# Two attention mixers of a decoder trunk: keys projected ahead of queries, odd values four heads at a time, a shorter inverse root

## The chip, the cores and the metric

One core of one Trainium2 chip runs the whole kernel in one launch. The metric is device time in microseconds (us), the median of three runs.

## The reference

A decoder of two layers on a sequence of 512 tokens of width 1024, all in float32. Each layer is half a SwiGLU feed-forward block (width 2816), a mixer, and half a feed-forward block again; each part reads a root-mean-square norm of the running sum `x` and adds to it.

```python
def rms_norm(x, g):
    y = x * rsqrt(mean(x * x, axis=-1) + 1e-6)
    return y * g

x = x + 0.5 * swiglu(rms_norm(x, ffn_pre_norm[l]), ...)
h = rms_norm(x, mix_norm[l])
x = x + even_mixer(h) if l == 0 else x + odd_mixer(h)
x = x + 0.5 * swiglu(rms_norm(x, ffn_post_norm[l]), ...)

# even: z = h @ w_in; 8 heads x 64 of causal attention (with 512 tokens and blocks of 256
#   every past block is chosen), beside a gated unit of 8 groups x 64; both -> w_out
# odd: 8 heads, each with two q/k maps of 64 and values of 128:
p = softmax(causal(q k^T / 8))          # for both maps
a = p[0] - lam * p[1]
o = rms_norm(a @ v, subln_g) * (1 - lambda_init)      # -> w_out
```

q and k of every head get a rotary embedding on their first 16 dimensions. A final norm ends it.

## The kernel before

`x` lies in SBUF as 8 tiles of 128 features x 512 tokens. Every float32 operand is split into a rounded high part and a low rest (`hi`, `lo`, the format is `fp32r`), and every product is three matmuls: high times high, high times low, low times high (`mm3`). A weight chunk of 128x1024 is loaded (`w_raw`), rounded on ACT (L128) and subtracted on DVE (L129).

All work is a list of slots. One slot is a projection or a part of one; for the mixers that is 24 matmuls of 512 columns (`project`) or, for the odd values, 48 of 256 columns. `st.later(n, fn)` hangs smaller work (a head's scores, transposes, the product with the values, a norm) n slots further on; `step()` emits what is due ahead of the slot's matmuls. This sets the order in which the code is written. The framework then schedules: it may put instructions that it reckons ready ahead of earlier ones on the same engine, and each engine runs its list in order. In the trace the matmuls of the output projection stand between a head's transposes, which the code writes in one block.

In a mixer `qk_slots` projects a pair (even: two heads; odd: the two maps of one head) in two slots, queries first, then keys. `rotated` (L839 to L842) applies the rotary embedding and hands the result to `Pair.q` or `Pair.k` one step later. `Pair.q` makes for each half of the rows a tile `qs` with the high part in the half's own 64 rows and the low part in the other 64. `Pair.k` makes for each half a tile `ks` that holds high and low of the keys in both 64-row halves: round (L862), subtract (L863), and one transfer on SP's queue from the half's own rows to the other 64 (L864). `Pair.scores` (L882, L883) then needs two matmuls per 128 queries.

Numbers of slots after the queries' and keys' pair: `EV` for the even mixer (scores, transposes, product with the values), `OD` for the odd one (scores of map 0, of map 1, transposes, product, sums of squares, row scale).

The odd values are projected for two heads at a time (`values(p)`, after heads 1, 3, 5 and 7), two slots each, into two PSUM banks. The output projection (`out_proj`) follows: three `begin` slots with the first half of the contraction, then `end_early`, which takes heads' results as they become available and emits the last heads' hung-on work between; six of the eight PSUM banks hold its sums then.

`rsqrt` (L205 to L221) is the inverse root without a table: a guess from the bits, a cubic step and a Newton step, ten DVE instructions; it runs 15 times (six norms, one layer norm, eight heads).

Of the kernel before, what the change touches and what calls it, by code (L numbers as in the profile page):

```python
# [18 lines left out]
P = 128  # L19
# [13 lines left out]
def trunk_kernel(ctx: ExitStack, tc: tile.TileContext, a, out):  # L33
# [6 lines left out]
    def bank(name):  # L40
        return ps.tile([P, 512], F32, name=name, tag="bank")
# [5 lines left out]
    def t2k(tag, name, dt=F32):  # L47
        return act.tile([P, T], dt, name=name, tag=tag, bufs=BUFS[tag])
# [7 lines left out]


    EB = 3
    EV = (3, 5, 6)
    OD = (3, 4, 6, 7, 9, 10)  # L60


    class Item:
# [141 lines left out]
    def rsqrt(dst, src, scale, n, plus=EPS):  # L205


        v, y, a, b = [sm.tile([P, n], F32, name=f"rs{i}") if n <= 32 else tmp(f"rs{i}") for i in range(4)]
        if isinstance(plus, float):
            nc.vector.tensor_scalar(v, src, scale, plus, op0=OP.mult, op1=OP.add)  # L210
        else:
            nc.vector.scalar_tensor_tensor(v, src, scale, plus, op0=OP.mult, op1=OP.add)
        nc.vector.tensor_scalar(y.bitcast(I32), v.bitcast(I32), -0.5, float(0x5F3759DF), op0=OP.mult, op1=OP.add)
        nc.vector.tensor_mul(a, y, y)
        nc.vector.tensor_mul(a, a, v)
        nc.vector.tensor_scalar(b, a, 0.375, -1.25, op0=OP.mult, op1=OP.add)
        nc.vector.tensor_mul(b, b, a)
        nc.vector.scalar_tensor_tensor(y, b, 1.875, y, op0=OP.add, op1=OP.mult)
        nc.vector.scalar_tensor_tensor(a, y, -0.5, y, op0=OP.mult, op1=OP.mult)
        nc.vector.tensor_mul(a, a, v)  # L220
        nc.vector.scalar_tensor_tensor(dst, a, 1.5, y, op0=OP.add, op1=OP.mult)  # L221


    class Norm:
# [607 lines left out]
    def two(name, dt=F32):  # L832
        return w4(name, dt)

    def rotated(pq, tables, place):

        cr, sr = tables
        sw, q = tmp("sw"), tmp("q")
        nc.vector.stream_shuffle(sw, pq, SWAP)  # L839
        nc.vector.tensor_mul(q, pq, cr)  # L840
        nc.vector.tensor_mul(sw, sw, sr)
        nc.vector.tensor_add(q, q, sw)  # L842
        st.mids.append(lambda: place(q))

    class Pair:
# [10 lines left out]
                self.QS.append(t)  # L856

        def k(self, k):
            for h in range(2):
                own, other = HALF[h], HALF[1 - h]  # L860
                t = two("ks", F32R)
                nc.scalar.activation(t[own, 0], k[own], AF.Copy)  # L862
                nc.vector.tensor_sub(t[own, 1], k[own], t[own, 0].bitcast(F32))  # L863
                nc.sync.dma_start(t[other].bitcast(F32), t[own].bitcast(F32))  # L864
                self.KH.append(t[:, 0])
                self.KL.append(t[:, 1])

        def scores(self, c, su, o, ebufs):

# [93 lines left out]
    def qk_slots(w, norm, tables, pair, hold, after):  # L963

        def fn(o):
            def go(ws):
                b = bank("pq")
                project(b, ws, norm)

                def evac():  # L970
                    rotated(b, tables(), pair.q if o == 0 else pair.k)
                    if o == 1:
                        after()
                if hold:
                    st.later(hold - o, evac)
                else:
                    evac()
            return go
        st.add([chunk(w[0])], fn(0))
        st.add([chunk(w[1])], fn(1))  # L980


    def even_mixer(norm, feed):
# [170 lines left out]
    def odd_mixer(norm, feed):  # L1154
# [22 lines left out]
        def head(h, pair):  # L1177

            keep = {}

            def s0():
                keep["su"] = sm.tile([P, 2 * TT], F32, name="su2")
                keep["e0"] = pair.scores(0, keep["su"], 0, EB)

            def s1():
                su = keep["su"]
                e0, e1 = keep["e0"], pair.scores(1, su, TT, EB)
                ratio = sm.tile([P, TT], F32, name="su")
                nc.vector.reciprocal(ratio, su[:, TT:])
                nc.vector.scalar_tensor_tensor(ratio, ratio, box["neg_lam"], su[:, :TT], op0=OP.mult, op1=OP.mult)  # L1190
                for i in range(TT):
                    nc.vector.scalar_tensor_tensor(e0[i], e1[i], ratio[:, i:i + 1], e0[i],
                                                   op0=OP.mult, op1=OP.add)
                nc.vector.scalar_tensor_tensor(box["eps"][:, :, h], su[:, :TT], EPS, su[:, :TT], op0=OP.mult, op1=OP.mult)

            def t():
                keep["pt"] = transposed(keep["e0"])

            def o():
                o_ = attend(box["v", h // 2], slice((h % 2) * P, (h % 2 + 1) * P), keep["pt"])  # L1200
                keep["o"] = t2k("r2", "o")
                nc.scalar.activation(keep["o"], o_, AF.Copy)
                sq = tmp("sq")
                nc.scalar.activation(sq, o_, AF.Square)
                keep["sq"] = sq

            def c():
                pc = bank("pc")
                for t in range(TT):
                    nc.tensor.matmul(pc[:, t:t + 1], keep["sq"][:, t * P:(t + 1) * P], ones1,  # L1210
                                     start=True, stop=True)
                keep["col"] = sm.tile([P, TT], F32, name="ocol")
                rsqrt(keep["col"], pc[:, :TT], 1.0 / P, TT, box["eps"][:, :, h])

            def r():
                row = bcast_row(keep["col"], "orow", True)
                on = keep["o"]
                nc.vector.scalar_tensor_tensor(on, on, box["sg"], row, op0=OP.mult, op1=OP.mult)
                if h < 2:
                    t = two("m", F32R)  # L1220
                    mh[h], ml[h] = split_into(t[:, 0], t[:, 1], on)
                else:
                    mh[h], ml[h] = split(on, "m", "h")

            for n, fn in zip(OD, (s0, s1, t, o, c, r)):
                st.later(n + int(fn is r and h < 7), fn)

        def values(p):
            b = []

            def half(n):
                def fn(w):
                    if n == 0:
                        b.extend(bank("pv") for _ in range(2))
                    for t in range(TT):
                        r = slice(t * P, (t + 1) * P)
                        o = b[t // 2][:, (t % 2) * 256:(t % 2 + 1) * 256]
                        for k in range(4 * n, 4 * n + 4):
                            s = slice((k % 4) * 256, (k % 4 + 1) * 256)
                            go = {"skip_group_check": True}  # L1240
                            nc.tensor.matmul(o, norm.hi[k][:, r], w[0][:, s], start=k == 0 and t % 2 == 0,
                                             stop=False, **go)
                            nc.tensor.matmul(o, norm.hi[k][:, r], w[1][:, s], start=False, stop=False, **go)
                            nc.tensor.matmul(o, norm.lo[k][:, r], w[0][:, s], start=False, stop=k == KT - 1, **go)
                    if n == 1:
                        evac()
                return fn

            def evac():
                halves = [t2k("h", "v", F32R).rearrange("p (n c) -> p n c", n=2) for _ in range(3)]  # L1250
                vh = [halves[t][:, 0] for t in range(TT - 1)]
                vl = [halves[t][:, 1] for t in range(TT - 1)]
                vw = t2k("h", "vw")[:, :256]
                for t in range(TT):
                    evac_value(t, b[t // 2][:, (t % 2) * 256:(t % 2 + 1) * 256], norm.col[:, t:t + 1], vh, vl, vw)
                box["v", p] = (vh, vl, vw)
            for n in range(2):
                st.add([chunk(a["ov"][p, n])], half(n))

        for h in range(8):  # L1260
            pair = Pair()
            if h == 0:
                n = len(st.slots)
                qk_slots(a["oqk"][h], norm, lambda: box["rope"], pair, 2,
                         lambda h=h, pair=pair: head(h, pair))
                first, end, fn, dense, raws = st.slots[n]
                st.slots[n] = (first, end, lambda ws, fn=fn: (begin(), fn(ws)), dense, raws)
            else:
                qk_slots(a["oqk"][h], norm, lambda: box["rope"], pair, 0,
                         lambda h=h, pair=pair: head(h, pair))  # L1270
            if h % 2 == 1:
                values(h // 2)
        out_proj(a["oo"], ([0, 1, 2, 3], [4, 5, 6, 7]), mh, ml, feed)

# [167 lines left out]
```

## Time and profile before

| | |
|---|---|
| median of 3 runs | 1815.01 us (1814.34 to 1815.54) |
| profiled execution | 1815.92 us |
| its span, first to last instruction | 1813.9 us |
| PE (matmul) busy | 1801.5 us, 12708 matmuls |
| DVE busy | 1553.2 us |
| ACT busy | 981.2 us |
| POOL busy | 177.2 us |
| mean granted TensorE clock | 0.998 of full |

A matmul's row gives its start and its duration with the drain of the array; successive ones overlap, so the step from start to start is what a matmul costs in a stream. The profiled execution lasted 2.0 us longer than its span, and 0.9 us longer than the median of the runs.

### The profile page before, as it was taken

Reading aid. Unit: us, or ns where it says so; the run is one execution under the profiler, and the core shown is the slowest. Engines: PE = TensorE matmul, PEld = TensorE weight load, DVE = VectorE, ACT = ScalarE, POOL = GpSimd, SP = SyncE. Lnnn points to the kernel's source line nnn. Section 1 sums busy time; section 2 is a strip of 40 time slices with the busy share of each in tenths; the row PEclk is TensorE's granted clock in tenths of the full one; section 3 lists DMA queues with packets and bytes.
Section 4 is the critical chain, followed back from the end, with each engine's and each line's share of the span. In section 5 each row is a group of like instructions: output and inputs, shape, how many; then the busy total and the mean of one; then the engine's idle time right before and its main releaser. Section 6 shows DMA issues by size and latency. Waiting matters only on the chain.

```text
span 1813.9 us, 32304 instructions
## 1 busy us (share of the span) xinstructions
PE 1801.5 (99%) x12708; PEld 1689.5 (93%) x12708; DVE 1553.2 (86%) x2554; ACT 981.2 (54%) x1577; POOL 177.2 (10%) x154
## 2 busy tenths in 40 slices
PE   9999999999999999999999999999999999999998
PEld 7999999888888999999899999998999889999997
DVE  8989898878868889898988989888999688898986
ACT  6545554544965545454654646455566455455544
POOL 0111110100000111110011111100000001111100
PEclk9999999999999999999999999999999999999999
DMA  7587876421325687875547878742333245878771
GB/s 244 128 222 168 221 167 170 142 96 59 117 82 148 153 224 163 223 160 151 170 115 187 201 188 201 187 132 90 94 94 94 93 138 130 221 169 220 169 179 62
DMA packets 150743, 279.87 MB, mean 154 GB/s; under 512 B 11840, under 2 KB 65728, under 8 KB 150592
## 3 DMA queue, kind: packets, MB, share of 16 engines
q1 hardware_dynamic: 111216, 209.62, 36.2%
q0 software_dynamic: 38080, 67.12, 22.8%
q8 instruction: 100, 1.64, 0.4%
q10 hardware_dynamic: 1296, 1.08, 0.2%
q14 instruction: 51, 0.42, 0.1%
HBM read 269.39 MB, written 2.10 MB: 150 GB/s over the span
## 4 chain that ended last, share of the span: by engine, by line
PE 96%; DVE 2%; ACT 1%; issue 0%; DMA 0%; SPq 0%; DVEq 0%
PE pA L417 11%; PE pA L416 11%; PE pA L415 11%; PE pD L415 6%; PE pD L417 6%; PE pD L416 6%; PE pB L417 3%; PE pB L416 3%; PE pB L415 3%; PE py L180 3%; PE py L182 3%; PE py L181 3%; PE pq L181 2%; PE pq L182 2%; PE pq L180 2%; PE pu L182 2%
## 5 line engine op out<-in xcount | busy, mean ns | idle before, releaser
L128 ACT ACTIVATE w_hi<-w_raw 128x1024 fp32r<-128x1024 f32 (+2 forms) x539 | 517.3, 968 | 430.1 <-DVE w_raw L378 122.6
L129 DVE TENSOR_TENSOR w_lo<-w_raw,w_hi 128x1024 fp32r<-128x1024 f32 (+2 forms) x539 | 599.1, 1113 | 135.7 <-ACT w_hi L128 99.5
L368 POOL DMA_DIRECT2D w_raw<-in_gu x72 | 87.4, 1215 | 1050.0 <-PE pu L182 229.3
L417 PE MATMUL pA<-xh,w_lo 128*128 128x256 f32 x576 | 163.1, 283 | 0.1
L415 PE MATMUL pA<-xh,w_hi 128*128 128x256 f32 x576 | 163.1, 283 | 0.0
L416 PE MATMUL pA<-xt,w_hi 128*128 128x256 f32 x576 | 163.0, 283 | 0.0
L415 PE MATMUL pA<-h,w_hi 128*128 128x256 f32 x576 | 163.0, 283 | 0.0
L416 PE MATMUL pA<-h,w_hi 128*128 128x256 f32 x576 | 163.0, 283 | 0.0
L417 PE MATMUL pA<-h,w_lo 128*128 128x256 f32 x576 | 163.0, 283 | 0.0
L415 PE MATMUL pA<-xt,w_hi 128*128 128x256 f32 x576 | 163.0, 283 | 0.0
L417 PE MATMUL pA<-xt,w_lo 128*128 128x256 f32 x576 | 163.0, 283 | 0.0
L416 PE MATMUL pA<-xl,w_hi 128*128 128x256 f32 x576 | 163.0, 283 | 0.0
L415 PEld LDWEIGHTS pA<-xh,w_hi 128*128 128x128 f32 x576 | 110.5, 192 | 0.8 <-ACT v L555 0.2
L417 PEld LDWEIGHTS pA<-xh,w_lo 128*128 128x128 f32 x576 | 110.5, 192 | 0.3 <-DVE w_lo L129 0.3
L378 DVE TENSOR_TENSOR w_raw<-w_raw 128x1024 f32<-128x1024 f32 (+1 forms) x100 | 109.4, 1094 | 1.5
L416 PEld LDWEIGHTS pA<-xl,w_hi 128*128 128x128 f32 x576 | 110.6, 192 | 0.2
L415 PEld LDWEIGHTS pA<-h,w_hi 128*128 128x128 f32 x576 | 110.6, 192 | 0.0
L416 PEld LDWEIGHTS pA<-h,w_hi 128*128 128x128 f32 x576 | 110.6, 192 | 0.0
L417 PEld LDWEIGHTS pA<-h,w_lo 128*128 128x128 f32 x576 | 110.6, 192 | 0.0
L417 PEld LDWEIGHTS pA<-xt,w_lo 128*128 128x128 f32 x576 | 110.6, 192 | 0.0
L416 PEld LDWEIGHTS pA<-xt,w_hi 128*128 128x128 f32 x576 | 110.6, 192 | 0.0
L415 PEld LDWEIGHTS pA<-xt,w_hi 128*128 128x128 f32 x576 | 110.6, 192 | 0.0
(297 smaller groups left out, 5356.8 us busy)
## 6 DMA issues: line engine op xcount, KB each, us to landing
w_raw<-in_gu SPq DMA_DIRECT2D x210, 512.0 KB, 4.5
w_raw<-in_gu POOLq DMA_DIRECT2D x92, 512.0 KB, 7.2
w_raw<-in_wd SPq DMA_DIRECT2D x120, 384.0 KB, 3.7
w_raw<-in_wd POOLq DMA_DIRECT2D x48, 384.0 KB, 5.8
w_raw<-in_wd SPq DMA_DIRECT2D x64, 128.0 KB, 2.5
w_raw<-in_oqk SPq DMA_DIRECT2D x16, 512.0 KB, 4.5
ks<-ks SPq DMA_DIRECT2D x24, 256.0 KB, 3.1
w_raw<-in_eqk SPq DMA_DIRECT2D x8, 512.0 KB, 3.4
```

The source lines that it names most:

```text
L128: self.rounded.append(nc.scalar.activation(hi, raw, AF.Copy))
L129: nc.vector.tensor_sub(lo, raw, hi.bitcast(F32))
L180: nc.tensor.matmul(o, sh, mh, start=first, stop=False)
L181: nc.tensor.matmul(o, sh, ml, start=False, stop=False)
L182: nc.tensor.matmul(o, sl, mh, start=False, stop=last)
L368: nc.gpsimd.dma_start(dst, src, accum_op=OP.add)
L378: return lambda: nc.vector.tensor_add(r[dst], r[dst], r[other])
L415: nc.tensor.matmul(o, w[0][:, s], t[0], start=new and p + j == 0, stop=False, **go)
L416: nc.tensor.matmul(o, w[0][:, s], t[1], start=False, stop=False, **go)
L417: nc.tensor.matmul(o, w[1][:, s], t[0], start=False, stop=p == self.n - 1, **go)
```

## The change

- `qk_slots` projects keys first, queries second.
- `Pair.k` splits all 128 rows at once (one ACT and one DVE instruction instead of two each) into a tile `t`; two transfers on SP's queue copy the second half's rows to both halves of a tile `u`, and a third, on POOL's queue, copies the first half's rows of `t` over its second half. Head or map 0 reads `t`, 1 reads `u`.
- `EV` and `OD` are one slot less throughout.
- The odd values are projected for four heads at a time, after heads 0 and 4, in four slots of 24 matmuls of 512 columns, into four PSUM banks. A weight chunk is gathered by four loads of 128x256 instead of one of 128x1024. The total number of slots is the same.
- `rsqrt` takes one step with a polynomial of degree four instead of a cubic and a Newton step: eight DVE instructions instead of ten.

```diff
-    EV = (3, 5, 6)
-    OD = (3, 4, 6, 7, 9, 10)
+    EV = (2, 4, 5)
+    OD = (2, 3, 5, 6, 8, 9)
...
-        nc.vector.tensor_scalar(y.bitcast(I32), v.bitcast(I32), -0.5, float(0x5F3759DF), op0=OP.mult, op1=OP.add)
+        nc.vector.tensor_scalar(y.bitcast(I32), v.bitcast(I32), -0.5, float(0x5F1A5380), op0=OP.mult, op1=OP.add)
         nc.vector.tensor_mul(a, y, y)
         nc.vector.tensor_mul(a, a, v)
-        nc.vector.tensor_scalar(b, a, 0.375, -1.25, op0=OP.mult, op1=OP.add)
-        nc.vector.tensor_mul(b, b, a)
-        nc.vector.scalar_tensor_tensor(y, b, 1.875, y, op0=OP.add, op1=OP.mult)
-        nc.vector.scalar_tensor_tensor(a, y, -0.5, y, op0=OP.mult, op1=OP.mult)
-        nc.vector.tensor_mul(a, a, v)
-        nc.vector.scalar_tensor_tensor(dst, a, 1.5, y, op0=OP.add, op1=OP.mult)
+        nc.vector.scalar_tensor_tensor(b, a, -3.85771995, a, op0=OP.add, op1=OP.mult)
+        nc.vector.scalar_tensor_tensor(b, b, 6.07466985, a, op0=OP.add, op1=OP.mult)
+        nc.vector.scalar_tensor_tensor(b, b, -5.05940212, a, op0=OP.add, op1=OP.mult)
+        nc.vector.scalar_tensor_tensor(dst, b, 2.84331969, y, op0=OP.add, op1=OP.mult)
...
         def k(self, k):
-            for h in range(2):
-                own, other = HALF[h], HALF[1 - h]
-                t = two("ks", F32R)
-                nc.scalar.activation(t[own, 0], k[own], AF.Copy)
-                nc.vector.tensor_sub(t[own, 1], k[own], t[own, 0].bitcast(F32))
-                nc.sync.dma_start(t[other].bitcast(F32), t[own].bitcast(F32))
+            t, u = two("ks", F32R), two("ks", F32R)
+            nc.scalar.activation(t[:, 0], k, AF.Copy)
+            nc.vector.tensor_sub(t[:, 1], k, t[:, 0].bitcast(F32))
+            a, b = HALF
+            nc.sync.dma_start(u[a].bitcast(F32), t[b].bitcast(F32))
+            nc.sync.dma_start(u[b].bitcast(F32), t[b].bitcast(F32))
+            nc.gpsimd.dma_start(t[b].bitcast(F32), t[a].bitcast(F32))
...
-                    rotated(b, tables(), pair.q if o == 0 else pair.k)
+                    rotated(b, tables(), pair.k if o == 0 else pair.q)
...
-        st.add([chunk(w[0])], fn(0))
-        st.add([chunk(w[1])], fn(1))
+        st.add([chunk(w[1])], fn(0))
+        st.add([chunk(w[0])], fn(1))
...
-                o_ = attend(box["v", h // 2], slice((h % 2) * P, (h % 2 + 1) * P), keep["pt"])
+                o_ = attend(box["v", h // 4], slice((h % 4) * P, (h % 4 + 1) * P), keep["pt"])
...
+                    for k in (2 * c, 2 * c + 1):
+                        s = slice(k % 2 * 512, k % 2 * 512 + 512)
+                        for t in range(TT):
+                            r = slice(t * P, (t + 1) * P)
+                            mm3(b[t], norm.hi[k][:, r], norm.lo[k][:, r], w[0][:, s], w[1][:, s],
+                                k == 0, k == KT - 1)
...
+            for c in range(4):
+                cols = [slice((2 * c + e) % 4 * 256, ((2 * c + e) % 4 + 1) * 256) for e in range(2)]
+                st.add([chunk(*[a["ov"][p, c // 2][:, s] for s in cols for p in (q, q + 1)])], part(c))
...
-            if h % 2 == 1:
+            if h in (0, 4):
                 values(h // 2)
```

## Rows read from the trace of the kernel before

**Rows 1.** The page: PE's busy time, and the chain that ended last.
```profile
PE 1801.5 (99%) x12708; PEld 1689.5 (93%) x12708; DVE 1553.2 (86%) x2554; ACT 981.2 (54%) x1577; POOL 177.2 (10%) x154
...
PE 96%; DVE 2%; ACT 1%; issue 0%; DMA 0%; SPq 0%; DVEq 0%
```

**Rows 2.** Whom PE waited for: total us, times, longest.
```profile
PE pq L181 <- DVE xl L237: 0.6, 1, 0.6
...
PE s L882 <- DVE ml L1139: 0.5, 1, 0.5
```

**Rows 3.** Busy time by engine in the two mixers: stretch, length, engines.
```profile
341.00:536.00 195.00, 194.53 (x963) 163.32 (x962) 146.71 (x298) 116.49 (x227) 6.15 (x4) 1.00 0.29 93
1215.00:1449.00 234.00, 233.43 (x1363) 205.84 (x1362) 198.00 (x501) 133.61 (x286) 2.53 (x2) 1.00 0.31 97
```

**Rows 4.** PE in time order, a value slot's first matmul and what follows it.
```profile
1249.37 0.28 PE L1241 MATMUL pv<-w_hi,xh 128*128 128x256 f32 x1
...
1255.12 0.28 PE L882 MATMUL s<-ks,qs 128*128 128x256 f32 x1
```

**Rows 5.** PE in time order, 18 matmuls of the even values, first and last.
```profile
401.08 0.39 PE L180 MATMUL pv<-w_hi,xh 128*128 128x512 f32 x1
...
404.94 0.39 PE L182 MATMUL pv<-w_hi,xl 128*128 128x512 f32 x1
```

**Rows 6.** PE in time order, two places near the even mixer's end.
```profile
487.89 0.34 PE L883 MATMUL s<-ks,qs 128*128 128x384 f32 x1
488.69 0.50 PE L882 MATMUL s<-ks,qs 128*128 128x512 f32 x1 [0.46 <-DVE ml L1139]
...
516.41 0.48 PE L182 MATMUL py<-mh,w_lo 128*128 128x512 f32 x1
516.90 0.50 PE L180 MATMUL py<-mh,w_hi 128*128 128x512 f32 x1
```

**Rows 7.** The instructions of the key tiles: ns min/median/max, and transfers' landing.
```profile
L862 ACT ACTIVATE ks<-q x24: 615/630/633, 437.2 to 1392.1; 64x512 fp32r<-64x512 f32 x24
L863 DVE TENSOR_TENSOR ks<-q,ks x24: 654/686/690, 437.8 to 1392.8; 64x512 fp32r<-64x512 f32 x24
L864 SPq DMA_DIRECT2D ks<-ks x24: 461/467/1007, 438.5 to 1393.5; - x24
...
DMA to landing us min/median/max: 2.8/3.1/4.0
```

**Rows 8.** DMA issues by queue: KB each, median us to landing.
```profile
w_raw<-in_wd SPq DMA_DIRECT2D x120, 384.0 KB, 3.7
w_raw<-in_wd POOLq DMA_DIRECT2D x48, 384.0 KB, 5.8
```

**Rows 9.** DVE in time order, two neighbours inside one inverse root.
```profile
1432.26 0.17 DVE L216 TENSOR_SCALAR rs<-rs 128x4 f32<-128x4 f32 x1
1432.46 0.16 DVE L217 TENSOR_TENSOR rs<-rs,rs 128x4 f32<-128x4 f32 x1
```

**Rows 10.** Second pair of the even mixer: its queries, keys (DVE), scores (PE).
```profile
444.25 1.40 DVE L855 TENSOR_TENSOR qs<-q,qs 64x512 fp32r<-64x512 f32 x2
...
451.93 1.37 DVE L863 TENSOR_TENSOR ks<-q,ks 64x512 fp32r<-64x512 f32 x2
...
458.18 0.36 PE L882 MATMUL s<-ks,qs 128*128 128x256 f32 x1
```

**Rows 11.** Last odd head: scores end, mixing (DVE), transposes, and its final split (DVE).
```profile
1413.02 0.40 PE L883 MATMUL s<-ks,qs 128*128 128x512 f32 x1
...
1417.67 1.94 DVE L1192 SCALAR_TENSOR_TENSOR e<-e,su 128x128 f32<-128x128 f32 x4
...
1426.46 0.93 PE L903 MATMUL pt<-ident,e 128*128 128x128 f32 x7
...
1442.60 0.69 DVE L336 TENSOR_TENSOR ml<-o,mh 128x512 fp32r<-128x512 f32 x1 [0.70 <-ACT mh L335]
```

**Rows 12.** Whom ACT waited for, one row of those on transfers.
```profile
ACT w_hi L128 <- DMA w_raw<-in_eqk: 1.6, 1, 1.6
```

More of the change, by code (lines that the diff above doesn't have):

```diff
@@ L858, in k @@
         def k(self, k):
-            for h in range(2):
-                own, other = HALF[h], HALF[1 - h]
-                t = two("ks", F32R)
-                nc.scalar.activation(t[own, 0], k[own], AF.Copy)
-                nc.vector.tensor_sub(t[own, 1], k[own], t[own, 0].bitcast(F32))
-                nc.sync.dma_start(t[other].bitcast(F32), t[own].bitcast(F32))
-                self.KH.append(t[:, 0])
-                self.KL.append(t[:, 1])
+            t, u = two("ks", F32R), two("ks", F32R)
[5 more added lines that the diff above has]
+            nc.gpsimd.dma_start(t[b].bitcast(F32), t[a].bitcast(F32))
+            for w in (t, u):
+                self.KH.append(w[:, 0])
+                self.KL.append(w[:, 1])
         def scores(self, c, su, o, ebufs):
@@ L1226, in head, with values, part @@
                 st.later(n + int(fn is r and h < 7), fn)
-        def values(p):
+        def values(q):
             b = []
-            def half(n):
+            def part(c):
                 def fn(w):
[L1233 to L1245, printed above, removed]
+                    if c == 0:
+                        b.extend(bank("pv") for _ in range(TT))
+                    for k in (2 * c, 2 * c + 1):
[4 more added lines that the diff above has]
+                                k == 0, k == KT - 1)
+                    if c == 3:
                         evac()
@@ L1249, in evac @@
             def evac():
[L1250 to L1253, printed above, removed]
+                vh = [t2k("h", "vh", F32R) for _ in range(TT - 1)]
+                vl = [t2k("h", "vl", F32R) for _ in range(TT - 1)]
+                vw = t2k("h", "vw")
                 for t in range(TT):
[L1255 to L1258, printed above, removed]
+                    evac_value(t, b[t], norm.col[:, t:t + 1], vh, vl, vw)
+                box["v", q // 2] = (vh, vl, vw)
+            for c in range(4):
+                cols = [slice((2 * c + e) % 4 * 256, ((2 * c + e) % 4 + 1) * 256) for e in range(2)]
+                st.add([chunk(*[a["ov"][p, c // 2][:, s] for s in cols for p in (q, q + 1)])], part(c))
         for h in range(8):
```

## The prediction, made before the change was run

> **What bounds the kernel now.** I read the page's busy times and chain first. PE is busy for 1801.5 of 1813.9 us and makes up 96% of the chain that ended last; no DMA and no other engine has more than 2% of it [rows 1]. But a busy PE is only a PE that holds a matmul, so the next view is whom PE waited for: of eight rows in all the two inside the mixers are 0.6 us at the odd mixer's start, for the norm's operand, and 0.5 us near the even mixer's end [rows 2]. The last view before the parts is the two mixers as stretches: PE is busy for 194.5 of 195 and 233.4 of 234 us at the full clock, DVE for 147 and 198 of them, POOL for 6 and 3 [rows 3]. So everything the change touches lies in 429 us in which PE has almost no hole. What shortens DVE, ACT or a chain between them is worth only the holes it closes; what takes PE's own time away is worth all of it; what opens a hole costs it in full.
>
> **Odd values: PE's own time.** Before: four pairs of heads x two slots x 48 matmuls = 384 of 256 columns. In the value slot shown the 48 take from 1249.37 to 1255.12, 119.8 ns each [rows 4]; 384 x 119.8 ns = 46.0 us. After: 2 x 4 x 24 = 192 of 512 columns. The same projection with 512 columns exists in the even mixer: 17 steps from 401.08 to 404.94, 227.1 ns each [rows 5]; 192 x 227.1 ns = 43.6 us. Saved: 2.4 us. I see no cover that could lose it, since PE has no hole to give it to; bounds 2.0 to 2.6, for steps a few ns off.
>
> The Trainium skill, "TensorE: Matmul & The Clock Gate", section "Back-to-back issue gap", puts a warm matmul at its columns over 2.4 GHz plus a fixed 2.5 ns; by that this edit would save an estimated 0.5 us only (384 x 109.2 ns less 192 x 215.8 ns). The trace differs from it: a 256-column matmul with its weight load takes 119.8 ns and not half of 227.1 ns [rows 4, 5], and the rows decide.
>
> The four loads per chunk instead of one cost SP 24 more issues at some 0.47 us [rows 7], 11 us in a 234 us stretch in which the DMA engines are busy for 0.31 [rows 3]; weight chunks are asked for two slots ahead, so 0. Without that cover it would be a wait of about one landing, 2.8 us at least [rows 7], at the first chunk. The values held in four banks over four slots leave four banks for scores and transposes; PE has the projection's own matmuls to run while a head waits for a bank, so 0, at worst some tenths.
>
> **Keys and inverse root: off the path.** One ACT and one DVE instruction less per pair, 12 pairs: 12 x 0.63 = 7.6 us of ACT and 12 x 0.686 = 8.2 us of DVE [rows 7]. The inverse root loses two of ten small DVE instructions that follow each other every 0.20 us [rows 9]: 15 x 0.4 = 6 us of DVE. Four-head evacuation of values saves some 1 us more. All of it lies beside PE's matmuls; PE waits for none of it but in the row of 0.5 us. Value 0; bounds 0 and -1, what PE's wait rows in the mixers hold together [rows 2].
>
> **Scores a slot sooner: the ends of the mixers.** In the middle of a mixer an earlier score changes nothing, since a projection always stands behind it. At the end the last heads' chains (scores, softmax, transposes, product, split) meet the output projection, which needs their results. In the even mixer two holes can be seen there: the third scores matmul follows its neighbour after 0.80 us where the neighbours take 0.18, a hole of 0.62; and 0.49 us stand between two 512-column matmuls, 0.26 more than 0.227 [rows 6]. With everything a slot earlier the last pair's second head has its result before its turn in `end_early`, and the crush for banks falls by a slot. I take both holes as closed, -0.9, rounded to -0.8; bounds 0 and -3 (the small gaps of some 0.09 us at each change between blocks add up to about that).
>
> The odd mixer's end moves the other way. Before, two value slots stood between head 7's projection and the output projection; after, the values are done earlier and nothing stands there. Counted in slots from `end_early`: head 7's transposes go from 0 to +1, its row scale from +4 to +5, head 6's from +3 to +4 and head 5's from -1 to +2. Is there still cover? Head 7's scores end at about 1413.4, its maps are mixed by 1417.67 + 1.94 = 1419.6, and its transposes begin at 1426.46: 6.9 us of slack. From the transposes to the final split, 1426.46 to 1443.3, 16.8 us pass [rows 11]. The matmuls of `end_early` and of the slot behind it that don't need head 7 are 4 x 3 x 3 + 2 x 3 x 3 = 54, at 0.227 us 12.3 us, plus transposes, products and sums of the last heads, about 6 us. That covers 16.8 us as before, but more of it now hangs on heads 5 and 6, which come later too. I take +0.5; bounds 0 and +1.5.
>
> **Keys over three transfers: the open price.** Keys move up a slot, scores too, so the keys have as long as before, but their way is longer. SP's first and second transfer go out 0.47 us apart and land 2.8 to 4.0 us after issue; the third overwrites rows that the first two read, so it waits for both, and it makes the tile that map 0 or head 0 needs first. No row shows a plain 256 KB transfer on POOL's queue; from below it is SP's 3.1 us [rows 7], from above POOL's 5.8 us for 384 KB, 2.1 us more than SP's 3.7 for the same size [rows 8]. So `t` is whole 0.5 + 2.8 + 3.1 = 6.4 to 0.5 + 4.0 + 5.8 = 10.3 us after its DVE subtraction, where 3.1 stood. In the even mixer's second pair the place of the first projection has its first subtraction at 444.94 and the place of the second is finished at 453.30; scores stood at 458.18 [rows 10]. With the roles swapped `t` is whole between 451.3 and 455.2, the queries at 453.3, and the scores, a slot of some 7 us sooner, would be due at about 451. Scores wait for the queries anyway until 453.3; the keys add between 0 and 1.9 us. Whether PE then stands still depends on whether the scheduler put other matmuls there. Nothing is queued behind the third transfer: POOL is busy for 2.5 us in the odd mixer [rows 3], and SP keeps its weight loads. Value 0, since the queries end last at the lower end and about the middle; bounds 0 and 12 x 1.9 = 23 us.
>
> **The sum.** 1815.9 of the profiled execution - 2.4 - 0.8 + 0.5 = 1813.2; the median of the runs lies 0.9 lower, so 1812.3, and I say 1812.4.
>
> **The rivals.**
> *Keys late (slower).* The scheduler reckons transfers too short, and PE, in order, stands at map 0's first scores matmul for POOL's transfer. For it: ACT did once stand 1.6 us for a weight load [rows 12], so the order does not always know landings. Against: PE never waited for a transfer in the mixers [rows 2]. If half of the 1.9 us shows in half of the 12 pairs, +5.7 us: 1818.1. It cancels the gain from 0.23 us per pair on (2.7 us in all), and decides for slower by 0.2% from 0.53 us per pair on. Its stretch: 1814.5 to 1824.
>
> The Trainium skill speaks against POOL's queue here: "SBUF — State Buffer", the box on DVE blocking DMA under "SBUF: two separate sides", says that a transfer issued by GpSimd gets no descriptors while DVE runs an instruction in a two-port mode. By that each third transfer could start later by the DVE instruction then running, an estimated 0.7 us, the length of a 512-column one [rows 7], inside the stretch just given; most DVE work of the mixers has two tensor operands, which the page excepts against such a write, and no run here shows a lock.
>
> *Both ends clean.* All small gaps of the even end go and the odd end costs nothing: -2.4 - 3 = 1809.6. For it: DVE is freed of 15 us. Against: the gaps come from blocks changing, not from waiting.
>
> *Nothing gained.* The odd end opens by its upper bound and the even end keeps its holes: -2.4 + 1.5 = 1814.1; or the 512-column values run no better than the page's estimate.
>
> **Chances.** Forecast 0.47 (1811 to 1814.5), keys late 0.26, both ends clean 0.15, nothing gained 0.12. The three runs before lie within 0.07%, and 0.2% (3.6 us) is about what a measurement of this kernel can tell from no change. Faster by more than that, under 1811.4: all of the clean ends and a third of the forecast's stretch, 0.30. Slower by more, above 1818.6: half of the late keys, 0.14. Same: 0.56. The range 1809.0 to 1818.5 leaves out the lower half of the clean ends and the upper half of the late keys, together under 0.2.
>
> **What would show it.** PE's matmuls fall from 12708 to 12516. A value slot's 24 matmuls step by 0.227 us. In PE's waits no row names `ks`. The hole in front of the third scores matmul near the even end is gone. DVE's busy time falls by some 15 us without a trace in the span. The forecast is wrong if PE's waits have a row for the transfer `ks<-ks`, if PE's idle time at the odd end goes above 2 us, or if the landing of POOL's transfers lies outside 3.1 to 5.8 us.

## The result, and the profile after

The changed kernel takes 1828.1 us (median of 6 runs, 1826.3 to 1830.2) beside 1815.7 us for the kernel before on the same chip: ratio 1.0072 [1.0061, 1.0082], 12.4 us slower. The forecast was 1812.4 us and its range ended at 1818.5. The profiled execution took 1827.05 us, with a span of 1825.2 us, 11.3 us more than before.

The page answers [rows 1] with PE's busy time and the chain, and then lists the transfers of the key tiles: bytes, and median us from issue to landing.

```profile
PE 1803.0 (99%) x12516; PEld 1681.2 (92%) x12516; DVE 1541.8 (84%) x2506; ACT 971.9 (53%) x1557; POOL 182.3 (10%) x166
...
PE 94%; DVE 3%; DMA 2%; issue 1%; ACT 0%; SPq 0%; POOL 0%; DVEq 0%; POOLq 0%; ACTq 0%
...
ks<-ks SPq DMA_DIRECT2D x24, 256.0 KB, 3.3
ks<-ks POOLq DMA_DIRECT2D x12, 256.0 KB, 4.7
```

PE has 192 matmuls fewer and yet 1.5 us more of busy time, so some of its matmuls ran slowly; and DMA, 0% of the chain before, has 2%. The view of whom PE waited for (total us, times, longest) has a new first row where [rows 2] had none on a transfer:

```profile
PE s L882 <- DMA ks<-ks: 8.8, 5, 3.4
...
PE pc L1210 <- ACT pw L912: 0.6, 1, 0.6
PE s L882 <- DVE qs L853: 0.5, 1, 0.5
```

To place it, I cut both mixers into three stretches: the even mixer's attention, the middle of the odd mixer, the odd mixer's end. The columns are stretch, length, busy time of PE, PEld, DVE, ACT and POOL, granted clock as a share of 2.4 GHz, DMA share. First the kernel before, then the one after.

```profile
425.00:545.00 120.00, 119.53 (x611) 100.53 (x610) 95.12 (x201) 84.37 (x183) 0.00 (x0) 1.00 0.30 94
1226.00:1385.00 159.00, 158.43 (x937) 140.60 (x936) 141.60 (x357) 91.75 (x202) 2.53 (x2) 1.00 0.28 86
1385.00:1475.00 90.00, 90.00 (x497) 77.79 (x497) 69.74 (x176) 48.98 (x99) 1.20 (x1) 1.00 0.34 112
```
```profile
425.00:545.00 120.00, 116.10 (x590) 98.26 (x589) 91.67 (x194) 82.50 (x178) 2.18 (x4) 0.99 0.33 101
1226.00:1385.00 159.00, 156.72 (x786) 132.24 (x786) 124.34 (x300) 80.49 (x170) 5.73 (x8) 1.00 0.32 95
1385.00:1475.00 90.00, 85.60 (x420) 71.10 (x420) 73.18 (x178) 51.85 (x108) 1.03 (x2) 0.98 0.35 112
```

Length less PE's busy time is PE's idle time: 0.47 + 0.57 + 0 = 1.0 us before, 3.90 + 2.28 + 4.40 = 10.6 us after, and in two stretches the clock has fallen. The first pair of the even mixer shows what happens there, in time order (start, duration, engine, line):

```profile
432.65 0.68 DVE L859 TENSOR_TENSOR ks<-q,ks 128x512 fp32r<-128x512 f32 x1
...
433.41 0.53 SPq L861 DMA_DIRECT2D ks<-ks  x1
...
433.99 0.59 SPq L862 DMA_DIRECT2D ks<-ks  x1
...
436.70 1.41 DVE L853 TENSOR_TENSOR qs<-q,qs 64x512 fp32r<-64x512 f32 x2 [0.70 <-ACT qs L852]
...
438.09 0.39 PE L182 MATMUL pq<-xh,w_lo 128*128 128x512 f32 x1
438.33 0.60 POOL L863 DMA_DIRECT2D ks<-ks  x1 [74.10 <-PE pq L181]
...
441.92 0.55 PE L882 MATMUL s<-ks,qs 128*128 128x256 f32 x1 [3.44 <-DMA ks<-ks]
```

The keys are split at 433.3 and the queries at 438.1. SP's two transfers go out at once; the second lands 3.7 us after its issue, at 437.7, and POOL sends the third 0.6 us later. It needs 3.5 us, and PE, whose queue has map 0's scores next, stands from the last projection matmul until then. The queries, which I had taken for the later operand, were 3.7 us sooner. From issue to landing, by line (min/median/max of 12 each; SP's first, SP's second, POOL's third):

```profile
DMA to landing us min/median/max: 2.8/2.9/2.9
...
DMA to landing us min/median/max: 3.7/3.7/3.9
...
DMA to landing us min/median/max: 3.4/4.7/5.7
```

So `t` is whole 8.4 to 10.6 us after its subtraction. Besides 441.92 the scores of map 0 or head 0 start behind such a landing at 1260.82, 1303.03, 1320.23, 1398.47 and 1417.37. Measured from start to start of the matmuls, less the usual step of the matmul before (0.227 us at 512 columns, 0.11 at 128), the six holes are 3.6 + 1.1 + 0.8 + 0.3 + 1.7 + 2.4 = 9.9 us; one more, 0.6 us at 458.63, waits for the queries.

The clock comes on top. Windows around the first pair's wait and the last head's (the granted clock is the third column from the end):

```profile
438.50:441.90 3.40, 0.00 (x0) 0.01 (x1) 3.40 (x6) 1.06 (x1) 0.43 (x1) 0.95 0.65 233
441.90:444.40 2.50, 2.48 (x8) 2.31 (x9) 2.46 (x8) 1.06 (x2) 0.00 (x0) 0.50 0.02 7
444.40:446.00 1.60, 1.60 (x7) 1.33 (x6) 1.30 (x3) 1.59 (x4) 0.00 (x0) 0.81 0.00 0
446.00:448.00 2.00, 2.00 (x10) 1.64 (x10) 0.18 (x1) 1.76 (x7) 0.00 (x0) 1.00 0.46 100
...
1417.80:1420.70 2.90, 2.90 (x10) 2.50 (x9) 2.45 (x9) 1.08 (x4) 0.00 (x0) 0.50 0.02 6
1420.70:1422.00 1.30, 1.30 (x6) 0.99 (x5) 1.30 (x6) 0.61 (x2) 0.00 (x0) 0.80 0.96 293
```

Behind each of these two waits PE runs for some 3 us at 1.2 GHz. Lost: 2.5 x 0.50 + 1.6 x 0.19 = 1.55 us and 2.9 x 0.50 + 1.3 x 0.20 = 1.7 us, together 3.3. The account: 9.5 us more idle, 3.3 us of clock, 2.4 us less for the odd values make +10.4 of the 11.3 us. The rest are gaps too small for this view, since a 512-column matmul is shown busy for 0.39 us and the next follows after 0.227.

### The profile page after: what moved, and what is told of

The parts are those of the page before. It is cut to its first block, busy times and chain, and to the rows that moved or that the text cites. A ratio compares the mean times of both kernels' runs of the same rounds, so it can differ in the third digit from the quotient of the medians.

```text
span 1825.2 us, 31944 instructions
## 1 busy us (share of the span) xinstructions
PE 1803.0 (99%) x12516; PEld 1681.2 (92%) x12516; DVE 1541.8 (84%) x2506; ACT 971.9 (53%) x1557; POOL 182.3 (10%) x166
## 4 chain that ended last, share of the span: by engine, by line
PE 94%; DVE 3%; DMA 2%; issue 1%; ACT 0%; SPq 0%; POOL 0%; DVEq 0%; POOLq 0%; ACTq 0%
PE pA L413 11%; PE pA L415 11%; PE pA L414 11%; PE pD L413 6%; PE pD L415 6%; PE pD L414 6%; PE pB L415 3%; PE pB L413 3%; PE pB L414 3%; PE py L180 3%; PE py L182 3%; PE py L181 3%; PE pq L181 2%; PE pq L180 2%; PE pq L182 2%; PE pu L181 2%
```

## The experiments

Two theories were weighed at first. "Late keys": the third transfer ends after the place that the order gives to the scores. "Sooner slots": giving scores, transposes and products an earlier slot opens the ends, whatever the transfers do. A third, "values", says that four-head values lay open the odd mixer's end. Every run has the kernel before beside it on the same chip. "Idle" is PE's idle time in the three stretches above, in their order (before: 0.5 + 0.6 + 0); the stretches have the same borders in every run.

**Map 0 reads the tile that is whole after one hop.** All transfers and slots of the change stay; only the roles of the two tiles are swapped, so that SP's pair of transfers fills the first-needed tile.

```diff
-            a, b = HALF
+            b, a = HALF
...
-            for w in (t, u):
+            for w in (u, t):
```

> The changed kernel, but the tile that the two SP transfers complete is the one that map 0 (head 0) reads, and the tile that waits for the third transfer serves map 1 (head 1), which is needed a slot later; same instructions, same number of transfers. Theory 'late keys' (PE stands in order at map 0's first scores matmul until the third transfer lands, 10.8 us in six places, and runs at half clock for some us after the two longest): the wait rows on ks go to under 1 us and the time falls to 1811 to 1815. Theory 'sooner slots' (the heads' work a slot sooner crowds DVE, ACT and the PSUM banks, whatever the transfers): little changes, 1824 to 1830.

Measured: 1815.9 us, ratio 1.0002 [0.9992, 1.0011]; idle 1.3 + 0.6 + 1.2, clock 1.00 in all three. The scores that stood until 441.92 start at 438.99 without a wait. PE's longest wait in these stretches is for queries, by its wait rows:

```profile
PE s L882 <- DVE qs L853: 1.3, 1, 1.3
```

The whole loss of 12 us goes with one swap of two tiles. "Late keys" stands, though the time is 0.9 us above what it expected, and "sooner slots" falls as the cause of the loss: the slots are as in the change.

**The change with the slots of before.**

```diff
-    EV = (2, 4, 5)
-    OD = (2, 3, 5, 6, 8, 9)
+    EV = (3, 5, 6)
+    OD = (3, 4, 6, 7, 9, 10)
```

> The changed kernel with the scores, transposes and so on at their old distances in slots (EV and OD as before); keys first, three transfers, values of four heads and the quartic stay. 'Late keys': the third transfer gains a slot of some 7 us, more than the longest wait of 3.6 us, so no wait on ks and 1812 to 1816, a little above the run with the swapped tiles because the odd end is a slot later. 'Sooner slots': also down to 1812 to 1816. Theory 'values' (moving the values ahead of head 7 opens the odd end): the odd end is worse by a slot, several us of PE idle there, 1818 to 1824.

Measured: 1825.1 us (the profiled execution 1822.9), ratio 1.0052 [1.0037, 1.0067]; idle 0.7 + 2.8 + 4.4. Of the key waits one is left, odd head 0; but the odd end has opened for other reasons:

```profile
PE py L180 <- ACT w_hi L128: 2.1, 1, 2.1
...
PE s L882 <- DMA ks<-ks: 1.5, 1, 1.5
PE pt L903 <- DVE pl L916: 1.5, 2, 1.3
```

Missed: "late keys" alone would have brought it back near the kernel before, and it lies 1.1 us above what "values" expected too. A slot more cures all key waits but one, and the odd end is open. So the four-head values seem to have a price of their own, which the next run takes alone.

**Four-head values alone, on the kernel before.** Keys, slots and inverse root are those of before.

```diff
-            if h % 2 == 1:
+            if h in (0, 4):
                 values(h // 2)
```

(with `values` and its evacuation as in the change)

> The kernel before with the odd values of four heads at a time alone; slots, keys and inverse root as before. 'Late keys' and 'sooner slots' expect the 2.4 us of matmul time gained, less what the odd end loses, 1812 to 1815. 'Values': 1818 or more, with PE idle at the odd end.

Measured: 1820.4 us, ratio 1.0025 [1.0014, 1.0037]; idle 0.5 + 1.5 + 3.3. Whom PE waited for in the last stretch:

```profile
PE py L180 <- DVE nm L889: 1.4, 1, 1.4
PE pt L903 <- DVE pl L916: 1.3, 1, 1.3
PE pc L1210 <- ACT pw L912: 0.6, 1, 0.6
```

PE in time order, where the last head's transposes and the norm's sums stand:

```profile
1432.93 0.55 PE L903 MATMUL pt<-ident,e 128*128 128x128 f32 x3 [1.31 <-DVE pl L916]
...
1434.72 1.86 PE L1210 MATMUL pc<-ones,sq 128*128 128x1 f32 x8 [0.61 <-ACT pw L912]
```

And the windows behind them (granted clock third from the end):

```profile
1434.00:1436.00 2.00, 1.39 (x8) 1.28 (x7) 1.02 (x2) 0.91 (x2) 0.00 (x0) 0.65 0.00 0
1436.00:1438.00 2.00, 2.00 (x7) 1.71 (x8) 1.27 (x6) 0.00 (x0) 0.00 (x0) 0.50 0.00 0
1438.00:1440.00 2.00, 2.00 (x10) 2.00 (x9) 0.88 (x6) 0.00 (x0) 0.00 (x0) 0.50 0.00 0
1440.00:1442.00 2.00, 2.00 (x10) 1.61 (x10) 0.28 (x1) 1.08 (x2) 0.00 (x0) 0.65 0.04 8
```

The time is as "values" expected. The span is 5.4 us longer although 2.4 us of matmul time are saved. The odd end pays 3.3 us of waits and up to 3.4 us of half clock behind them (2 x 0.35 + 2 x 0.5 + 2 x 0.5 + 2 x 0.35); the middle another 0.9. Each of the three waits ends with an instruction that reads a PSUM bank (`nm` comes with the reading of the scores, `pl` and `pw` are read from the transposes) and that writes nothing the waiting matmul reads. By the kernel's operands, then, PE waits there for a bank to come free.

**Keys alone, on the kernel before**: keys first, three transfers, sooner slots; values in pairs at their old places.

```diff
-    EV = (3, 5, 6)
-    OD = (3, 4, 6, 7, 9, 10)
+    EV = (2, 4, 5)
+    OD = (2, 3, 5, 6, 8, 9)
...
-        st.add([chunk(w[0])], fn(0))
-        st.add([chunk(w[1])], fn(1))
+        st.add([chunk(w[1])], fn(0))
+        st.add([chunk(w[0])], fn(1))
```

(with `Pair.k` and the order of the rotations as in the change)

> The kernel before with the keys' part alone: keys first, 128-row split, three transfers, scores a slot sooner; values in pairs of heads and the old inverse root. 'Late keys': PE's wait rows on ks of 6 to 12 us in all, 1824 to 1832, that is 10 to 16 us over before. 'Sooner slots' expects the same time but with PE's waits named after DVE, ACT or banks. 'Values': about the time of before.

Measured: 1833.8 us, ratio 1.0100 [1.0085, 1.0116], slower than the whole change and 1.8 us above what "late keys" expected; idle 4.7 + 10.1 + 1.5. The largest part is one hole at the odd mixer's head 0:

```profile
1253.46 0.59 SPq L864 DMA_DIRECT2D ks<-ks  x1
...
1257.66 0.60 POOL L865 DMA_DIRECT2D ks<-ks  x1 [10.35 <-DVE sw L841]
...
1254.53 0.39 PE L182 MATMUL pq<-xh,w_lo 128*128 128x512 f32 x1
1264.43 0.55 PE L884 MATMUL s<-ks,qs 128*128 128x256 f32 x1 [9.51 <-DMA ks<-ks]
```

PE's other two holes of over 1 us, 4.2 us at 442.04 and 1.5 us at 1417.19, also end 0.1 us behind the landing of a third transfer, though the wait rows name DVE for them. With pairs, the first value slots come only after head 1, and in the trace only the 48 matmuls of head 1's projections stand in front of head 0's scores. In the whole change 74 matmuls of the values stand there, and 1.1 us of waiting is left. The parts lean on each other.

**The change with the old two transfers** (`Pair.k` as before, keys first and slots sooner kept).

```diff
-            t, u = two("ks", F32R), two("ks", F32R)
...
-            nc.gpsimd.dma_start(t[b].bitcast(F32), t[a].bitcast(F32))
+            for h in range(2):
+                own, other = HALF[h], HALF[1 - h]
...
+                nc.sync.dma_start(t[other].bitcast(F32), t[own].bitcast(F32))
```

> The changed kernel with the keys' old layout (two half splits, two independent SP transfers of one hop), all else as changed. 'Late keys': both tiles land one hop after their split, no wait on ks, 1813 to 1817, like the run with the tiles exchanged. If the 128-row split or the third transfer's traffic itself helped, this run would lie above that one by more than 0.1%.

Measured: 1816.8 us, ratio 1.0012 [1.0003, 1.0022]; idle 1.8 + 1.4 + 1.8, and no row of PE's waits names `ks`. It confirms the one-hop run: without a tile that needs two transfers one after the other the loss is gone, but for a tenth of a per cent. Whether the 128-row split helps by itself can't be told from it: the two runs are 0.1% apart, and their intervals overlap.

**The third transfer on SP's queue.**

```diff
-            nc.gpsimd.dma_start(t[b].bitcast(F32), t[a].bitcast(F32))
+            nc.sync.dma_start(t[b].bitcast(F32), t[a].bitcast(F32))
```

> The changed kernel with the third transfer on SP's queue instead of POOL's. If the length of the chain is what costs ('late keys'), SP's issue and landing of some 3.7 us instead of POOL's 0.6 + 4.7 takes about 1.6 us from each of six waits: waits on ks of 3 to 5 us in all, 1819 to 1823, unless SP, which then stands for the first two landings, holds weight loads back. If POOL's queue as such were the cause (descriptors held up while DVE runs), the waits would go entirely, under 1816.

Measured: 1822.1 us, ratio 1.0044 [1.0030, 1.0058]; idle 3.7 + 1.4 + 2.3. Issue to landing of the third transfer, by its line:

```profile
DMA to landing us min/median/max: 2.9/4.6/6.2
```

And the first pair in time order:

```profile
437.39 0.47 SPq L863 DMA_DIRECT2D ks<-ks  x1
...
441.66 0.35 PE L882 MATMUL s<-ks,qs 128*128 128x256 f32 x1 [3.70 <-DMA ks<-ks]
```

SP issues 0.1 us after the second landing (433.47 + 3.8) where POOL took 0.6, but the median landing time stays the same, 4.6 beside 4.7. The first pair still stands for 3.7 us, and head 2's scores start at 1301.02, 0.1 us behind a third landing, after 0.9 us that the wait rows put down to DVE. The run is 7.5 us over its kernel before, so 4.9 of the 12.4 us are gone. That fits the issue: over the twelve pairs POOL's came 0.6 to 0.8 us behind the second landing, SP's at most 0.14 us. But single landings moved too (the last head's third transfer took 4.3 us, not 5.7), so the share of the issue is not shown. The larger part of the loss stays with the second hop, whoever sends it. The Trainium skill, "DMA: Bandwidth & Descriptors", section "Issuing engines are not separate DMA queues", says that transfers share the same engines whoever issues them, and another issuer saves only sequencer time; the two medians agree. The Trainium skill's box on DVE blocking DMA ("SBUF — State Buffer"), which the prediction weighed, is neither needed nor shown by this run.

**One hop first, with values in pairs at their old places** (the one-hop kernel with the values of before).

```diff
-            if h in (0, 4):
+            if h % 2 == 1:
                 values(h // 2)
```

> The run with the exchanged tiles, but the odd values in pairs of heads at their old places (after heads 1, 3, 5, 7). 'Values at the odd end': 2.4 us of matmul time come back and some 2 us of gaps at the odd end go, 1813 to 1816. If the earlier slots open the ends by themselves, above 1817.

Measured: 1819.0 us, ratio 1.0022 [1.0013, 1.0031]; idle 1.3 + 2.8 + 0. Missed, high by some 3 us: the odd end is clean again, but head 0 waits even for the tile of one hop.

```profile
1249.45 0.59 SPq L862 DMA_DIRECT2D ks<-ks  x1
...
1250.53 0.39 PE L182 MATMUL pq<-xh,w_lo 128*128 128x512 f32 x1
1253.19 0.36 PE L882 MATMUL s<-ks,qs 128*128 128x256 f32 x1 [2.27 <-DMA ks<-ks]
```

The transfer lands 3.6 us after its issue, at 1253.1. PE reaches these scores behind the 48 matmuls of head 1's projections; with the value slots after head 0 it reached them behind 59 value matmuls, and there was no wait. So the value slots after head 0 are what hides the keys of head 0, in the change too.

**One hop first, heads 0 to 3 four at a time, the last four heads in pairs.** This puts cover on both ends: value slots after head 0, and after heads 5 and 7.

```diff
-            if h in (0, 4):
-                values(h // 2)
+            if h == 0:
+                values(0)
+            elif h in (5, 7):
+                pair_values(h // 2)
```

> The run with the exchanged tiles, with values of heads 0 to 3 four at a time (512 columns, after head 0) and those of 4, 5 and of 6, 7 in pairs after heads 5 and 7, so that two value slots stand between head 7 and the output projection again. Half of the matmul saving (1.2 us) without the odd end's gaps: 1811.5 to 1814, below both kernels.

Measured: 1814.6 us, ratio 0.9998 [0.9989, 1.0008]; idle 1.3 + 1.3 + 0. The span, 1812.4 us, is the shortest of all runs, 1.5 us under that of before; the interval cannot tell it from no change. Missed by 0.6 us: 1811.5 to 1814, below both kernels, was expected, and head 0 still waits 0.7 us for its keys. It is the best form of the change that was found.

**The same mix of values on the kernel before** (slots and keys of before, four-head values after head 1, pairs after heads 5 and 7).

```diff
-            if h % 2 == 1:
-                values(h // 2)
+            if h == 1:
+                values(0)
+            elif h in (5, 7):
+                pair_values(h // 2)
```

> The kernel before with the values of heads 0 to 3 four at a time after head 1 and those of 4, 5 and 6, 7 in pairs after heads 5 and 7; keys, slots and inverse root as before. By the matmul steps 1.2 us less than before, 1813.3 to 1814.2 where before is 1814.7; if the four banks cost something in the middle too, the same as before or above.

Measured: 1814.7 us beside 1815.5, ratio 0.9998 [0.9989, 1.0007], span 1812.8; idle 0.5 + 1.0 + 0. The median is 0.8 us lower and the span 1.1 us shorter, where half of the 2.4 us of values would be 1.2; the interval cannot tell it from no change. PE idles 0.4 us more in the middle, so four heads at a time cost little where nothing ends behind them.

**Pairs, but the last pair's values early, on the kernel before.** It asks whether the price of the four-head values is their place.

```diff
-            if h % 2 == 1:
+            if h in (1, 3, 5):
                 values(h // 2)
+            if h == 5:
+                values(3)
```

> The kernel before with one thing moved: the values of heads 6 and 7 are projected after head 5 (still in pairs, 256 columns), so that no value slot stands between head 7 and the output projection. 'Cover at the odd end' (the two value slots behind head 7 hide its chain, and the loss of the values-alone run comes from their place): 6 to 9 us slower than before, 1821 to 1824, with PE's gaps between 1400 and 1450. Rival 'four banks' (the loss comes from the four banks and the wider values): about the time of before, 1814 to 1816.

Measured: 1817.8 us beside 1815.5, ratio 1.0014 [1.0005, 1.0023]; span +2.8 us; idle 0.5 + 0.6 + 1.1. The odd end's waits:

```profile
PE pc L1210 <- ACT sq L1204: 0.7, 1, 0.7
PE py L181 <- DVE ml L336: 0.4, 1, 0.4
```

Missed in size: taking the two value slots from the end costs 2.8 us, not the 6 and more that cover alone would have to explain. In the run with four-head values alone there are 2.2 us more of waits and up to 3.4 us of half clock behind them, which this run doesn't have (clock 1.00 in all three stretches). The waits also differ in kind: here PE waits for operands (`sq`, `ml`), there for banks. The four banks that the values hold can't be the reason, since the last of them was read out by 1353.2 in that run, 52 us before the first of those waits. That the last three heads follow each other there without a value slot fits, but no run shows it alone.

**The quartic alone, on the kernel before.**

```diff
-        nc.vector.tensor_scalar(b, a, 0.375, -1.25, op0=OP.mult, op1=OP.add)
...
+        nc.vector.scalar_tensor_tensor(dst, b, 2.84331969, y, op0=OP.add, op1=OP.mult)
```

> The kernel before with the shorter inverse root alone. All theories: it lies beside PE's work, within 0.1% of before; the rival that the shorter chains close gaps gives 1 us or more.

Measured: 1815.0 us beside 1815.5, ratio 0.9998 [0.9989, 1.0007], span 1813.9 as before. The inverse root has no effect here that a run could show.

## Why the prediction was wrong

**Keys over three transfers, value 0: the step that failed.** Its bounds were nearly right: `t` whole 6.4 to 10.3 us after the subtraction, measured 8.4 to 10.6. What failed is the sentence behind them, "value 0, since the queries end last at the lower end and about the middle". That was worked out for the second pair of the even mixer, with a lead of the keys over the queries of 8.4 us (444.94 to 453.30), and for that pair it held: in the change its queries end at 458.6, its `t` is whole at 454.3. But it was taken for all twelve pairs. In the change the lead, from the keys' subtraction to that of the first queries, is 0.8 to 12.6 us, and `t` comes after these queries in ten pairs. In six of the ten PE had reached the scores by then: in five, the scheduler's order had put them only some 1 to 2 us behind the queries' end. The rival "keys late" had the mechanism, POOL's transfer in front of map 0's first scores, at 5.7 us and a chance of 0.26. The price was more than twice that. The places were six, as supposed, but each wait was 1.6 us on average and up to 3.6, not half of 1.9: 9.9 us together; and 3.3 us of half clock came behind them, a term that stood nowhere. Swapping the two tiles gives 12 us back (1815.9 beside 1828.1).

**Head 0 of the odd mixer** was left out altogether. There queries and keys are rotated in the same slot, so no lead of the keys over the queries exists. It costs 1.1 us in the change, where value slots stand in front of its scores, and 9.5 where they don't.

**The odd mixer's end, +0.5 with bounds 0 and +1.5: right in size, in part by luck.** Of the 4.4 us of idle time there 3.8 are key waits, so 0.6 is left; with one hop first it is 1.2. But on the slots of before the four-head values cost 3.3 us of waits and 3.4 of clock in this stretch. That the slots that come sooner pay for it fits; no run changes them alone. I had counted cover in slots and microseconds of matmuls, and 54 matmuls were enough in sum; the waits for PSUM banks, which make up those 3.3 us, were not in the working of this end.

**Right.** The odd values: 12516 matmuls, and the 192 of 512 columns follow each other every 0.227 us, which is the term of -2.4 us. The estimate by the formula of the Trainium skill, "TensorE: Matmul & The Clock Gate", section "Back-to-back issue gap", is 0.216 us. That section gives the formula for a matmul by itself, which the prediction left out when it used it for a stream; the trace's step is 0.011 us longer. The even end, -0.8: from 470 to 545 us PE's idle time falls from 0.47 to 0, the one wait of 0.5 us in front of the third scores matmul being gone; but the even mixer's second pair waits 0.5 us for its queries in the change, and 1.3 us with one hop first. Keys' evacuation and inverse root, 0: DVE is busy for 11.4 us less (some 15 foreseen), and the inverse root alone leaves the span as it was; the evacuation was not run alone. Nothing was queued behind the third transfer, as said; PE itself was what stood. The stretch from 470 us, before and after:

```profile
470.00:545.00 75.00, 74.53 (x385) 62.08 (x384) 52.85 (x113) 54.90 (x122) 0.00 (x0) 1.00 0.28 93
...
470.00:545.00 75.00, 75.00 (x389) 63.44 (x388) 54.64 (x114) 55.57 (x121) 0.83 (x2) 1.00 0.31 100
```

**The forecast's own tests.** "A row for the transfer `ks<-ks`" in PE's waits is there, the first. PE's idle time at the odd end, 4.4 us, is above the 2 us named. POOL's landings, 3.4 to 5.7 us, lie inside 3.1 to 5.8. The sum as it came out: -2.4 for the values, -0.5 at the even end, +10.0 for all other idle time of PE in the three stretches, keys before all, and +3.3 for the clock make 10.4 of the 11.3 us.

## What to carry to other kernels

When a tile's way gets one dependent transfer longer, work out its landing at the upper bound for every place it is used, not for one, and look at what PE's queue has in front of its first reader; a bound that reaches past the other operand is not worth 0 where the engine takes its work in order. If two tiles are whole at different times, let the first reader have the sooner one: that was the whole loss here. And add to a wait of PE the slow stretch that can stand behind it, and price an edit that takes slots of matmuls from a stretch with what was ending under them.

## What the runs showed of the hardware

- PE's clock fell to 1.2 GHz for some 3 us behind waits of 3.4 us and 2.2 us in the change, and for up to 6.8 us (granted clock 0.65, 0.50, 0.50 and 0.65 in the four windows from 1434 to 1442) behind two waits of 1.3 and 0.6 us in the run with four-head values alone; behind one of 1.5 us at 1398.47, and behind one of 2.3 us at 1253.19 in the run with one hop first and the old values, it stayed at 2.4 GHz. So the length of one wait does not decide it. The matmuls at once behind the wait can still be fast: in the run with the third transfer on SP the first four, of 256 columns, start 0.12 to 0.20 us apart, and two of 512 columns after them 0.43 us, where 0.227 is the step at full clock. The Trainium skill, "TensorE: Matmul & The Clock Gate", section "HAM oscillation — how this bites in real kernels", tells of matmuls throttled behind a wait for a transfer; the first two cases agree, the last, also a wait for a transfer, does not.
- A 256 KB transfer from SBUF to SBUF took, from issue to landing, 2.8 to 2.9 us as SP's first of a pair and 3.7 to 3.9 us as its second in the change; the third took 3.4 to 5.7 us when POOL issued it (median 4.7) and 2.9 to 6.2 us when SP did (4.6). SP's issue came 0.1 us after the landing that it waited for, POOL's 0.6 us, in the first pair.
